# Work woven between attention steps: after every step, or after every other step twice as much at a time

## The chip, the core and the metric

The kernel runs on one core of a Trainium2 chip. A core has five engines that each follow their own list of instructions in order: TensorE (PE in the profile) multiplies matrices, VectorE (DVE) and ScalarE (ACT) work element by element and along rows, GpSimd (POOL) does elementwise work as well, and SyncE (SP) issues the transfers between the main memory and the on-chip memory. TensorE writes its results into PSUM, a small memory that VectorE and ScalarE read from. An instruction waits for the results of other engines through semaphores. The metric is the device time of one execution in microseconds, less is better; the time before is the median of three runs, 1912.97 us (1905.94 to 1915.4).

## What is computed

A two-layer network over 512 latent tokens and 256 context tokens, 1024 channels each. Layer 0 mixes the tokens by attention, layer 1 by a state-space scan in both directions; each is followed by a gated feed-forward part with a short convolution. The change touches the attention of layer 0 alone:

```python
q_l, k_l, v_l = jnp.split(h_lat @ w_qkv, [Q_DIM, Q_DIM + KV_DIM], axis=-1)
q_l = rms_norm(q_l.reshape(bsz, seq, N_HEADS, HEAD_DIM), q_norm)
...
q_l = apply_rope(q_l, cos, sin)
...
s = jnp.einsum('bqhgd,bkhd->bhgqk', q, k).astype(jnp.float32) * (HEAD_DIM ** -0.5)
p = jax.nn.softmax(s, axis=-1).astype(v.dtype)
return jnp.einsum('bhgqk,bkhd->bqhgd', p, v)
...
x = x + mod_l[2] * o_l
```

There are 16 query heads of width 64 and 4 key heads, each shared by four query heads. Latent queries look at all 768 keys, context queries at the 256 context keys. The output goes through a square projection w_o, and before it every sub-layer is normalised and modulated (shift, scale and gate) by a linear map of the conditioning vector.

## The kernel before

Channels lie on the 128 partitions and tokens along the rows. Numbers are f32; a product that needs the precision is made from three products of a high and a low half (`mm3`: high by high, high by low, low by high), so weights are loaded and split into halves first (`load_w`: a transfer, a copy on ScalarE, a difference on VectorE or GpSimd).

Attention (`attention`, from line 379) begins with a stretch whose order is written by hand. It makes the keys and the first four pairs of queries as raw products. The remaining order comes from a scheduler that places instructions engine by engine in keeping with their dependencies; the order in which the program states them is its guide.

Then the heads run in eight pairs (`Pair`), two heads side by side on the two halves of the partitions. A pair has seven steps (`steps`, lines 628 to 690): steps 0 to 5 take the 512 latent queries against one block of 128 keys, step 6 takes the 256 context queries against the two context blocks. Each step has the following parts.

- Scores `ps_s` (lines 673 and 675): three products of halves, and a fourth that subtracts each query's maximum by way of a diagonal matrix `diag`.
- The exponential `pr` on ScalarE (676), which reads the scores out of PSUM, and the running sum `acc` on VectorE (681, 683, 687).
- The values `ps_o` (637), a product of the exponentials with the values. It is stated one step late (`later_lat`, `later_ctx`), so that the next step's scores go ahead of it on TensorE. At the pair's end the sums `ps_sum` or `ps_oc` (643) follow, and three operations on VectorE that divide (648 to 650).

Between these, each step takes one piece of the next pair's `maxima` (lines 591 to 626): a first product `ps_m` (601) whose row maxima VectorE takes (603), to build the next pair's `diag` (619, 624). `ps_s` and `ps_m` take turns in two PSUM buffers of the tag S; each is freed when the exponential or the maximum has read it. All other PSUM results use four buffers of the tag B.

After each step, `fill.run(us)` (line 761) weaves in other work. `Fill` holds a queue of generators; each advances by a small piece when asked and says how many microseconds of TensorE the piece holds, or returns BREAK when its next piece needs something that is still under way. `run` adds its budget to what is left of an overdraft (a surplus is dropped), goes through the queue in order and advances the generators until the budget is used. A generator that returned BREAK cools: it is left out until its count, which goes down by one with each call of `run`, is used up.

The queue holds, in an order written out by hand, the preparation of the queries of pairs 1 to 7 (`queries`), the second half of the keys (`keys`), and six pieces of the modulation (`ada`). A preparation is a product `ps_q` (pairs 4 to 7 only, 105 to 108), then `normed`: squares on ScalarE (528), an exchange of halves by four transfers `qsw` (532), three operations on GpSimd (533 to 535), sums of squares by a matmul with two output columns `ssq` (236), their inverse root on VectorE and ScalarE (239 to 247), transposes `rsTq` (253) and multiplications on VectorE (539), and last the split into halves (85, 87). A BREAK stands between these groups. A modulation piece is a transfer `wada` of four tiles, a product `ps_ada` (128), a copy, and small products with two output columns `ps_adt` (134). At the start of pair p, `fill.require` states whatever is left of the preparation of pair p + 1. At the start of pair 6 the pieces of the output projection (`project`: transfers of w_o, products `ps_d`, sums into X on line 784) are added. The last pair's values go through the projection after the loop.

Of the kernel before, what the change touches and what calls it, by code (L numbers as in the profile page):

```python
# [175 lines left out]
class Fill:  # L176
# [1 line left out]


    def __init__(self):  # L180
        self.q, self.cool, self.left = [], {}, 0.0

    def add(self, gen):
        self.q.append(gen)
# [1 line left out]
    def run(self, us):  # L186

        self.left = min(self.left, 0.0) + us
        self.cool = {g: n - 1 for g, n in self.cool.items() if n > 1}
        for g in list(self.q):  # L190
            while self.left > 0 and g not in self.cool:
                r = next(g, None)
                if r is None:
                    self.q.remove(g)
                    break
                if r is BREAK:
                    self.cool[g] = 3
                    self.left -= 1.0
                else:
                    self.left -= r  # L200
# [178 lines left out]
def attention(g, fill, X, late):  # L379
# [336 lines left out]
    def osplit(p):  # L716
        hl_, hc_ = htiles(g, L, f"ol{p}"), htiles(g, C, f"oc{p}")
        o = g.o[p]
        if p < 6:
            o = t3(g, f"od{p}")  # L720
            nc.sync.dma_start(o, odram[p])
        split(g, o[:, :L], *hl_)
        split(g, o[:, L:T], *hc_)
        g.oT.append((hl_, hc_))
# [15 lines left out]
    for p in range(NH // 2):  # L740
        m = iter(())
        if p < 7:
            fill.require(qgen[p + 1])
            if p == 3:
                fill.require(kgen)
            m = pairs[p + 1].maxima()
        us = 1.75 if p < 6 else 2.9
        for t, todo in enumerate(pairs[p].steps()):
            next(m, None)
            if late_step:  # L750
                late_step()
            late_step = todo
            if t == 0:
                if p == 6:
                    for i in range(5):
                        osplit(i)
                    late()
            if p == 7 and t == 3:
                osplit(5)
                osplit(6)  # L760
            fill.run(us)
    late_step()
    osplit(7)

# [490 lines left out]
def body(nc, tc, I, out, dbg=None):  # L1255
# [47 lines left out]
    def late():  # L1303
        for fs in ((0, 1, 2), (3, 4), (5, 6, 7))[:-1]:
            fill.add(project(fs))

    attention(g, fill, X, late)
    fill.drain()
    g.tables = True
# [136 lines left out]
```

## Time and profile before

| | before |
|---|---|
| time of three runs, median | 1912.97 us |
| time of three runs, lowest and highest | 1905.94 and 1915.4 us |
| time of the profiled execution | 1914.7 us |
| span of the profiled execution, first to last instruction | 1912.9 us |
| mean clock granted to TensorE | 0.994 |
| the heads' loop in the span | 118.4 to 392.5 us |
| executions of the exponential of line 676 (eight pairs, seven steps) | 56 |

The profile is one execution, recorded by the hardware. In a timeline a row gives the start in microseconds, the length, the engine, the line of the kernel, the operation, the result and its sources by the program's names (buffer numbers left out), shapes and how many instructions the row merges; square brackets hold the idle time ahead of the row and what ended it. A row of the table of windows gives the bounds, the width, then the busy time of TensorE's matmuls, of its weight loads, of VectorE, ScalarE and GpSimd, each with its number of instructions, then the granted clock as a share of full speed, the share of the transfer engines and the gigabytes per second. A group of instructions has its count, the busy time in all, the mean length in nanoseconds, and the idle time ahead with what ended it. A matmul of two f32 operands stands in the trace as two. Matmuls are pipelined: a row's length holds its way through the array as well, so the distance from one start to the next is the better measure of what one costs.

### The profile page before, as it was taken

The page shows a single profiled execution, that of the slowest core. Times are in us where ns is not written, and L with a number is a line of the kernel's source. Part 1 is how long each engine was busy: PE and PEld are TensorE (multiplying, and loading weights), DVE is VectorE, ACT ScalarE, POOL GpSimd, SP SyncE. Part 2 cuts the span into 40 slices and gives each one's busy share as a digit, 9 for nine tenths or more (in the row PEclk, how much of TensorE's full clock was granted, in tenths as well). Part 3 has the DMA queues.
Part 4 walks back from the last instruction along what each step waited for, and adds up shares of the span by engine and source line. Part 5 has one row for each costly group of instructions (what it writes and reads, how often), then busy time and mean ns, then how long its engine had stood idle before and what let it go on. Part 6 is the DMA issues. An engine that isn't in the chain of part 4 may idle for free.

```text
span 1912.9 us, 27512 instructions
## 1 busy us (share of the span) xinstructions
PE 1876.5 (98%) x10834; PEld 1547.6 (81%) x10834; DVE 1311.2 (69%) x1943; ACT 823.0 (43%) x1426; POOL 309.8 (16%) x274
## 2 busy tenths in 40 slices
PE   9999999999999999999999999999999999999999
PEld 7866555678888888888888888888888878888887
DVE  5578778678877777444488777777888466565555
ACT  3634444255122222222266777776667352323331
POOL 2241111031000000000040344443434210000000
PEclk9989998999999999999999999999999999999999
DMA  9221332114434555221122443334443322323232
GB/s 337 78 89 45 113 112 95 34 45 166 132 122 132 174 188 166 66 67 60 62 89 87 121 118 115 126 113 133 120 138 115 91 77 86 102 88 110 88 100 88
DMA packets 73425, 210.02 MB, mean 110 GB/s; under 512 B 8912, under 2 KB 14416, under 8 KB 73168
## 3 DMA queue, kind: packets, MB, share of 16 engines
q1 hardware_dynamic: 73296, 208.26, 34.3%
q8 instruction: 85, 1.39, 0.3%
q14 instruction: 44, 0.36, 0.1%
HBM read 198.79 MB, written 6.82 MB: 107 GB/s over the span
## 4 chain that ended last, share of the span: by engine, by line
PE 79%; DVE 9%; issue 3%; ACT 2%; POOL 1%; DMA 1%; DVEq 0%; SPq 0%; POOLq 0%; ACTq 0%
PE ps_up L106 10%; PE ps_up L108 10%; PE ps_up L105 10%; PE ps_d L105 6%; PE ps_d L106 6%; PE ps_d L108 6%; PE ps_in L106 4%; PE ps_in L108 4%; PE ps_in L105 4%; PE ps_o L637 2%; PE ps_s L673 2%; PE ps_st L1033 2%; DVE ht L281 1%; PE ps_wo L108 1%; PE ps_wo L105 1%
## 5 line engine op out<-in xcount | busy, mean ns | idle before, releaser
L87 DVE TENSOR_TENSOR wl<-wst,wh 128x1024 fp32r<-128x1024 f32 x205 | 254.5, 1242 | 244.9 <-PE ps_up L106 137.7
L85 ACT CAST wh<-wst 128x1024 fp32r<-128x1024 f32 x211 | 221.2, 1049 | 423.2 <-DMA wst<-in_wup 333.8
L106 PE MATMUL ps_up<-hlf,wh 128*128 128x512 f32 x1008 | 357.0, 354 | 0.0
L105 PE MATMUL ps_up<-hhf,wh 128*128 128x512 f32 x1008 | 356.9, 354 | 0.0
L108 PE MATMUL ps_up<-hhf,wl 128*128 128x512 f32 x1008 | 356.8, 354 | 0.0
L105 PEld LDWEIGHTS ps_up<-hhf,wh 128*128 128x128 f32 x1008 | 190.5, 189 | 26.5
L106 PEld LDWEIGHTS ps_up<-hlf,wh 128*128 128x128 f32 x1008 | 190.6, 189 | 26.4
L108 PEld LDWEIGHTS ps_up<-hhf,wl 128*128 128x128 f32 x1008 | 190.5, 189 | 26.4
L105 PE MATMUL ps_in<-hhs,wh 128*128 128x512 f32 (+1 forms) x560 | 204.4, 365 | 0.0
L106 PE MATMUL ps_in<-hls,wh 128*128 128x512 f32 (+1 forms) x560 | 199.4, 356 | 0.0
L108 PE MATMUL ps_in<-hhs,wl 128*128 128x512 f32 (+1 forms) x560 | 198.7, 355 | 0.0
L105 PE MATMUL ps_d<-hdh,wh 128*128 128x512 f32 (+1 forms) x568 | 193.6, 343 | 1.4 <-DVE X L784 1.2
L108 PE MATMUL ps_d<-hdh,wl 128*128 128x512 f32 (+1 forms) x568 | 193.5, 341 | 0.0
L106 PE MATMUL ps_d<-hdl,wh 128*128 128x512 f32 (+1 forms) x568 | 193.0, 340 | 0.3 <-DVE hdl L87 0.3
L784 DVE SCALAR_TENSOR_TENSOR X<-ps_d,mod,X 128x512 f32<-128x512 f32 (+1 forms) x224 | 124.6, 583 | 36.9 <-PE ps_d L108 36.6
L106 PEld LDWEIGHTS ps_d<-hdl,wh 128*128 128x128 f32 x568 | 106.6, 188 | 14.8 <-DVE hdl L87 0.7
L105 PEld LDWEIGHTS ps_d<-hdh,wh 128*128 128x128 f32 x568 | 106.3, 188 | 14.8 <-DVE X L784 1.4
L105 PEld LDWEIGHTS ps_in<-hhs,wh 128*128 128x128 f32 x560 | 105.9, 189 | 15.1 <-issue 1.2
L108 PEld LDWEIGHTS ps_in<-hhs,wl 128*128 128x128 f32 x560 | 105.8, 189 | 14.8
L108 PEld LDWEIGHTS ps_d<-hdh,wl 128*128 128x128 f32 x568 | 106.7, 188 | 13.1
L106 PEld LDWEIGHTS ps_in<-hls,wh 128*128 128x128 f32 x560 | 106.0, 189 | 13.2
L676 ACT ACTIVATE pr<-ps_s 128x1024 f32<-128x1024 f32 x56 | 57.2, 1021 | 110.6 <-PE ps_s L675 109.6
(340 smaller groups left out, 3547.3 us busy)
## 6 DMA issues: line engine op xcount, KB each, us to landing
wst<-in_wup SPq DMA_DIRECT2D x88, 512.0 KB, 3.6
wada<-in_adaT SPq DMA_DIRECT2D x56, 512.0 KB, 3.9
wst<-in_win SPq DMA_DIRECT2D x48, 512.0 KB, 3.7
wst<-in_wdown SPq DMA_DIRECT2D x44, 512.0 KB, 3.6
E<-ad SPq DMA_DIRECT2D x64, 256.0 KB, 6.8
wada<-in_adaB SPq DMA_DIRECT2D x24, 512.0 KB, 4.6
ec<-ead SPq DMA_DIRECT2D x64, 128.0 KB, 5.0
wst<-in_wout SPq DMA_DIRECT2D x16, 512.0 KB, 3.6
```

What stands on the lines that cost most here:

```text
L85: keep(nc.scalar.copy(hi, src))
L87: keep(eng.tensor_tensor(lo, src, _r(hi), ALU.subtract))
L105: mm(out, wh, ah, start=first, stop=False)
L106: mm(out, wh, al, start=False, stop=False)
L108: mm(out, wl, ah, start=False, stop=last)
L281: nc.vector.scalar_tensor_tensor(t[:, c0:c1], ap, g.moda[layer][ca][:, m, v : v + 1], rs[:, c0:c1], ALU.mult, ALU.mult)
L637: nc.tensor.matmul(po[S64[e], :n], v, pr[:, 512 * e + off : 512 * e + off + n], start=first, stop=last)
L673: nc.tensor.matmul(outs[e], a[S64[e], k], b[S64[e], q], start=i == 0, stop=False)
L676: nc.scalar.activation(pr, ps, AF.Exp)
L784: nc.vector.scalar_tensor_tensor(ap, o[:, c0:c1], gate[:, m, v : v + 1], ap, ALU.mult, ALU.add)
L1033: nc.tensor.matmul(ps[:, d * 256 : (d + 1) * 256], Bt[:, t * P : (t + 1) * P], xw[d][t], start=t == ts[0], stop=t == ts[-1])
```

## The change

The cooling count becomes a field of the object, 2 in place of 3. In the loop, work is woven in after the steps 1, 3 and 5 of a pair with twice the budget, and after step 6 with the single one; after the steps 0, 2 and 4 none is. The budgets per pair are 7 x 1.75 = 12.25 us in pairs 0 to 5 (3 x 3.5 + 1.75 in the changed kernel) and 7 x 2.9 = 20.3 us in pairs 6 and 7 (3 x 5.8 + 2.9), the same sum both ways. The count goes down with each call of `run`, of which a pair now has four.

```diff
--- before.py
+++ after.py
@@ -178,7 +178,7 @@
     def __init__(self):
-        self.q, self.cool, self.left = [], {}, 0.0
+        self.q, self.cool, self.left, self.pause = [], {}, 0.0, 2
 
@@ -194,7 +194,7 @@
                 if r is BREAK:
-                    self.cool[g] = 3
+                    self.cool[g] = self.pause
                     self.left -= 1.0
@@ -758,7 +758,8 @@
             if p == 7 and t == 3:
                 osplit(5)
                 osplit(6)
-            fill.run(us)
+            if t % 2 or t == 6:
+                fill.run(us if t == 6 else 2 * us)
     late_step()
     osplit(7)
```

## The prediction

> **What bounds the kernel now.** I read the page first, then the busy times of the heads' stretch, then that stretch instruction by instruction on TensorE, ScalarE and VectorE, and last the granted clock in short windows.
>
> ```profile
> span 1912.9 us, 27512 instructions
> PE 1876.5 (98%) x10834; PEld 1547.6 (81%) x10834; DVE 1311.2 (69%) x1943; ACT 823.0 (43%) x1426; POOL 309.8 (16%) x274
> 118.40:392.50 274.10, 270.41 (x1662) 161.08 (x1662) 211.70 (x305) 114.01 (x157) 39.74 (x23) 0.97 0.25 83
> ```
>
> The profiled execution took 1914.7 us, 1.8 us more than its span of 1912.9 us; the median of the three runs is 1912.97 us, 1.7 us below it. I make the sum against this execution and carry the difference to the median. TensorE is busy for 98% of the span. The change acts only between 118.4 and 392.5 us (the last row: eight pairs of heads, seven steps each), where TensorE is busy for 270.4 of 274.1 us. So the woven work fills no large hole; it is itself work of the bounding engine, and its total does not change. What can change is the small change around it: switches between kinds of matmul, waits of a fraction of a microsecond, and the clock, which stands at 0.97 here.
>
> One ordinary step, on TensorE, then the other two engines:
>
> ```profile
> 159.42 0.50 PE L673 MATMUL ps_s<-qh,kh 64*128 64x512 f32 x2
> 160.45 0.40 PE L601 MATMUL ps_m<-kh,qh 64*128 64x512 f32 x2
> 160.77 1.08 PE L637 MATMUL ps_o<-pr,v 128*64 128x512 f32 x4
> 161.78 0.50 PE L105 MATMUL ps_q<-hha,wh 128*128 128x512 f32 x1
> 162.12 0.39 PE L106 MATMUL ps_q<-hla,wh 128*128 128x512 f32 x1
> ...
> 163.73 0.39 PE L108 MATMUL ps_q<-hha,wl 128*128 128x512 f32 x1
> 164.05 0.50 PE L673 MATMUL ps_s<-qh,kh 64*128 64x512 f32 x2
> 160.65 1.02 ACT L676 ACTIVATE pr<-ps_s 128x1024 f32<-128x1024 f32 x1 [3.18 <-PE ps_s L675]
> 160.88 1.23 DVE L603 TENSOR_REDUCE ma<-ps_m 128x2 f32<-128x1024 f32 x1 [0.75 <-PE ps_m L601]
> 162.03 1.21 DVE L683 TENSOR_TENSOR acc<-acc,pr 128x1024 f32<-128x1024 f32 x1
> ```
>
> Scores (ps_s) run from 159.42 to 160.45, the maxima of the next pair (ps_m) to 160.77, the values of the step before (ps_o) to 161.78: 2.36 us. Then come nine woven matmuls (ps_q), and the next scores begin at 164.05. ScalarE's exponential ends at 161.67, VectorE's maximum and sum (1.23 + 1.21) at 163.24.
>
> The clock (third number from the end) in windows cut at its changes, and at one place that has none:
>
> ```profile
> 92.80:96.20 3.40, 2.39 (x19) 1.84 (x18) 2.50 (x4) 2.52 (x3) 0.00 (x0) 1.00 0.00 0
> 96.20:99.70 3.50, 3.50 (x18) 3.50 (x19) 0.99 (x3) 1.29 (x3) 0.00 (x0) 0.51 0.32 77
> 120.10:123.50 3.40, 3.06 (x26) 2.49 (x25) 2.96 (x4) 3.27 (x6) 3.40 (x3) 1.00 0.50 155
> 123.50:130.40 6.90, 6.90 (x29) 2.54 (x29) 5.50 (x9) 3.26 (x6) 0.80 (x1) 0.51 0.44 125
> 178.10:181.50 3.40, 3.40 (x22) 2.32 (x19) 3.28 (x8) 1.04 (x3) 2.08 (x2) 1.00 0.00 0
> 287.40:290.80 3.40, 2.98 (x22) 2.09 (x20) 3.23 (x2) 1.06 (x2) 3.35 (x2) 1.00 1.02 399
> 291.00:301.30 10.30, 10.30 (x39) 6.09 (x39) 6.88 (x12) 3.29 (x5) 2.17 (x1) 0.51 0.27 105
> 294.20:297.60 3.40, 3.40 (x17) 3.38 (x18) 2.60 (x5) 0.28 (x1) 0.00 (x0) 0.50 0.00 0
> 96.00:97.00 1.00, 1.00 (x7) 1.00 (x7) 1.00 (x2) 0.00 (x0) 0.00 (x0) 0.62 0.26 61
> 123.00:124.00 1.00, 1.00 (x7) 1.00 (x8) 1.00 (x1) 1.00 (x2) 1.00 (x1) 0.77 0.00 0
> 290.00:291.00 1.00, 0.38 (x6) 0.01 (x2) 1.00 (x2) 0.00 (x0) 0.94 (x1) 0.90 1.02 399
> ```
>
> It is full or half. The mean of 0.62 from 96 to 97 puts the first drop at 97 − 0.38/0.5 = 96.24; in the same way the others begin at 123.54 and 290.80. The 27.30 and 167.26 us between them are 8 and 49 times 3.41 us; they last about 3.4, 6.9 and 10.2 us, that is 1, 2 and 3 such periods. So in this trace the clock is set anew every 3.41 us. What went ahead of each drop:
>
> ```profile
> 93.84 0.50 PE L601 MATMUL ps_m<-kh,qh 64*128 64x256 f32 x4 [1.01 <-ACT qh L85]
> 95.14 1.75 PE L236 MATMUL ssq<-cst,qsq 128*128 128x2 f32 x12
> 119.80 1.50 PE L236 MATMUL ssq<-cst,qsq 128*128 128x2 f32 x12
> 122.99 2.24 PE L236 MATMUL ssq<-cst,qsq 128*128 128x2 f32 x12 [0.34 <-ACT qsq L528]
> 178.75 1.50 PE L236 MATMUL ssq<-cst,qsq 128*128 128x2 f32 x12
> 287.74 1.50 PE L236 MATMUL ssq<-cst,qsq 128*128 128x2 f32 x12
> 290.99 0.80 PE L601 MATMUL ps_m<-kh,qh 64*128 64x256 f32 x4 [0.62 <-DVE ma L603]
> 293.62 3.58 PE L134 MATMUL ps_adt<-cst,ada_sb 128*128 128x2 f32 x16
> ```
>
> Matmuls with two output columns (ssq, the sums of squares; ps_adt, the turned modulation rows) stream almost nothing. Counted with the idle time, the periods before the drops hold 1.01 + 1.10 = 2.1, 1.1 + 0.34 + 0.55 = 2.0 and 1.43 + 0.43 = 1.86 us of near-idleness (a group of twelve ssq takes 1.43, from 119.80 to the next matmul at 121.23). The period from 178.15 holds one such group and is followed by no drop. The threshold lies between 1.43 and 1.86 us of 3.41.
>
> **The change part by part.** The built order of the changed kernel holds the same work in the stretch; it stands elsewhere. I count 18 steps with nothing woven in (the first, third and fifth of a pair mostly) against 2 before, so 16 new light steps, and as much more work in the heavy ones.
>
> *The switch.* A change of the kind of matmul costs the first one extra: the first ps_q takes 162.12 − 161.78 = 0.34 where a following one takes 0.23 (+0.11); the last ps_q holds until 164.05, 0.32 for 0.23 (+0.09). A light step saves both and pays one switch from values to scores (estimated +0.10, the mean of the two). 16 x −0.10 = −1.6 us; between 0 and −3.2.
>
> *A light step by itself.* Without the nine matmuls the next scores begin at 2.36 + 0.09 = 2.45 us after the last. Their bank was freed by the exponential, 161.67 − 159.42 = 2.25 us after: covered by 0.2. The next maxima need the bank that VectorE's maximum freed at 162.11, 2.69 us after, and come at 2.45 + 1.03 = 3.48: covered by 0.79. VectorE needs 2.3 us (start to start) of 2.45. So a light step runs without a wait as long as no more than about 0.8 us of woven work stands on VectorE ahead of its maximum. One step has no values to cover it: the first of all.
>
> ```profile
> 119.68 1.02 ACT L676 ACTIVATE pr<-ps_s 128x1024 f32<-128x1024 f32 x1 [0.75 <-PE ps_s L675]
> ```
>
> There the sums of squares stood behind the maxima (119.80, above); in the changed order the second scores follow at once and wait for the exponential to 120.70: +0.9 us.
>
> *VectorE's backlog.* Present waits of the maxima for VectorE:
>
> ```profile
> 138.95 0.50 PE L601 MATMUL ps_m<-kh,qh 64*128 64x512 f32 x2 [0.48 <-DVE mb L603]
> 306.97 0.50 PE L601 MATMUL ps_m<-kh,qh 64*128 64x256 f32 x4 [0.55 <-DVE ma L603]
> L601 PE MATMUL ps_m<-kh,qh 64*128 64x256 f32 (+1 forms) x140 | 21.3, 342 | 2.5 <-DVE ma L603 2.1 <-DVE mb L603 0.5
> ```
>
> Each is about 0.5 us, 2.5 us in all. Twice as much woven work at a time can put its normalisation in front of the light step's maximum, and no woven matmul covers TensorE then. Bounds: none of the 16 waits (0) and all wait 0.5 us (8.0). I take a third, +2.6 us, nearer the low end: in most steps the scheduler has put the normalisation behind the maximum.
>
> *The clock.* Before, the two drops cost 6.9 x 0.49 = 3.4 and 10.2 x 0.5 = 5.1, together 8.5 us. The first goes: the two ssq groups that shared a period now have a light step, or scores, between them (2.9 us of work from end to start), so with the 1.43 us of one group no period reaches 1.86. The second goes as it was, but all twelve ps_adt matmuls of the sixth pair (24 in the trace, two for each) now stand in one row: at 0.12 us each (the ssq group, 12 in 1.43) 2.9 us without streaming. Wherever the period's edge falls, it holds at least 1.65 us of them in about 9 of 10 cases. That drop lasts one or two periods: 1.7 or 3.4 us, I take 2.6. For ssq groups that meet a new wait I add 0.4 of a two-period drop, 1.4 us. Sum after 4.0, so −4.5 us; bounds −8.5 (no drop) and +8.5 (two-period drops at five places, 17.0).
>
> The Trainium skill, "TensorE: Matmul & The Clock Gate", section "HAM oscillation — how this bites in real kernels", has the abstract rule that only idle gaps over about 3.4 us bring the half clock; here the longest gap before a drop was 1.01 us, so the trace does not follow it. Its section "A second HAM failure mode: psum-queue depth-cycling" says that frequent micro-idling between groups of matmuls is enough, which speaks against this change; the trace agrees as far as 1.86 us in 3.41 goes.
>
> *Later preparation.* The cool time is now 2 runs of every second step, so 3 to 4 steps instead of 3, and the last pair's sums of squares move from the sixth pair's third step to its sixth, all its transposes to the seventh. Behind them stand VectorE's multiplications, ScalarE's high half of the queries, and the maxima of the last pair; behind these the scores that need the same banks.
>
> ```profile
> 306.83 0.68 DVE L539 TENSOR_TENSOR qs<-qs,rsTq 128x512 f32<-128x512 f32 x1
> 309.98 0.42 DVE L539 TENSOR_TENSOR qs<-qs,rsTq 128x256 f32<-128x256 f32 x1
> 310.61 0.81 ACT L85 CAST qh<-qs 128x768 fp32r<-128x768 f32 x1
> wst<-in_w_o SPq DMA_DIRECT2D x8, 512.0 KB, 4.5
> ```
>
> The chain is 0.68 + 0.42 + 0.81 = 1.9 us if nothing stands between, against scores and values of one step as cover, 1.03 + 1.01; but the pair's own closing work on VectorE stands between. Bounds 0 and 2.4 (one maximum and one sum ahead of the chain, 1.2 us each); I take +1.0. On SP's queue five of the last projection's loads now stand ahead of that pair's exchange of halves, which the multiplications need. One behind another they would take 5 x 4.5 = 22 us; the steps three to six that lie between are about 14 (2.9 of ps_adt and 1.43 of ssq on four steps of 2.45). They overlap, so I take nothing, and 8 us in the range.
>
> From the last step of the last pair on the order is the same on every engine, so no later stage should change in length.
>
> Sum: −1.6 + 0.9 + 2.6 − 4.5 + 1.0 = −1.6 us. 1914.7 − 1.6 = 1913.1 for a profiled execution, 1911 us for the median.
>
> **The rivals.**
> 1. *VectorE's backlog decides (slower).* Place: the maxima of the 16 light steps. Each waits 0.5 to 1 us and the waits join with ssq into more slow periods. Price: 8.0 (all wait 0.5) in place of 2.6, and three more two-period drops, 10.2: 1911 + 5.4 + 10.2 = 1927. It passes 0.5% (1922.5) from a mean wait of 0.88 us without more drops (16 x 0.88 = 14.1, 11.5 more than my 2.6), or 0.5 us with two more. For it: VectorE has 2.3 us of work in a step of 2.45, and is busy 211.7 of 274.1 us already. Against it: the 0.79 us of cover, and present steps that are uneven already, with 2.5 us of such waits in all.
> 2. *No drop at all (faster).* The rows of ps_adt count as activity, or are broken up by the edge. −1.6 + 0.9 − 8.5 = −9.2 with no backlog, and −11.7 if the present 2.5 us go as well: 1901 to 1904. For it: 178.1 shows that 1.43 us are borne. Against it: 294.20, a period full of ps_adt and scores, stayed at half. By the rule of the Trainium skill quoted above (no gap near 3.4 us) it would come out this way.
> 3. *Late preparation shows at every pair's end.* 7 x 1.0 us in place of 1.0: 1917. Against it: in the first, fifth and sixth pair the last transposes stand in the last step before as after.
> 4. *The change does little of what it says,* because the scheduler pulls woven matmuls back between the scores (it does so in the first and third pair): near 1913, inside the forecast.
>
> **How the numbers follow.** 0.5% of 1912.97 is 9.6 us, about what a measurement of this kernel can tell from no change; the three runs differ by as much. The forecast with rival 4 has 0.45, rival 3 0.12 (both within), rival 1 0.26 (all slower), rival 2 0.17 (counted as faster). The likeliest's own range is 1904 to 1919. The range of eighty in a hundred reaches to most of both outer cases: 1901 to 1926.
>
> **What would show it.** Right: in the heads' stretch light steps of 2.4 to 2.7 us and heavy ones of 5 to 8; no half clock around 123 us, and one of 3.4 or 6.8 us behind the row of ps_adt; waits of the maxima for VectorE of about 5 us in all; the stretch within 3 us of 274. Wrong: waits of the maxima over 10 us, more than two half-clock stays, scores that wait for the exponential in many steps (the cover of 0.2 us is thin), or a stage after 392 us that changes length.

## The result and the profile after

The changed kernel takes 1916.34 us (median of 20 runs, 1912.01 to 1921.7), the kernel before 1909.21 us (median of the 20 runs beside them). One of those 20 took 3066.82 us; the ratio compares fast runs alone. It is 1.0038, 95% interval [1.0028, 1.0048]: slower by 0.38%, about 7 us. That lies inside the predicted range and inside the 0.5% called no change, but the forecast of a small gain has the wrong sign.

The page of the profile after (its time is 1918.66 us, 1.8 us more than its span):

```profile
span 1916.9 us, 27524 instructions
PE 1875.7 (98%) x10834; PEld 1550.7 (81%) x10834; DVE 1314.3 (69%) x1943; ACT 823.7 (43%) x1426; POOL 309.6 (16%) x274
```

TensorE still bounds the kernel, with as much work as before. The window of the heads' stretch, after the change (columns as in the prediction):

```profile
118.50:395.40 276.90, 268.00 (x1662) 161.93 (x1661) 213.68 (x305) 114.38 (x157) 39.31 (x24) 0.98 0.25 82
```

The stretch is longer by 2.8 us (276.9 for 274.1) though its clock is better (0.98 for 0.97): it loses 5.1 us to half clock where the one before lost 8.5. Without these it is 6.2 us longer. Behind the stretch TensorE runs the same list in both kernels. One row of it, before and after:

```profile
1538.99 0.51 PE L105 MATMUL ps_first<-hhf,wh 128*128 128x256 f32 x2 [0.64 <-ACT hhf L290]
```

```profile
1541.85 0.50 PE L105 MATMUL ps_first<-hhf,wh 128*128 128x256 f32 x2 [0.64 <-ACT hhf L290]
```

The kernel after is 2.86 us late here and 4.00 us late at the last matmul (1913.33 for 1909.33). So the later stages take the same time but for 1.14 us, and these come from a drop of the clock close behind this row, which the profile before does not have. Two periods of 3.41 us before, then two after:

```profile
103.07:106.48 3.41, 1.62 (x16) 1.56 (x15) 3.41 (x3) 0.00 (x0) 0.97 (x1) 1.00 0.00 0
1540.07:1543.48 3.41, 2.12 (x16) 1.71 (x15) 3.41 (x5) 1.78 (x6) 2.34 (x2) 1.00 0.31 123
```

```profile
1540.93:1544.34 3.41, 2.02 (x11) 1.20 (x9) 3.41 (x8) 3.05 (x7) 0.82 (x1) 1.00 0.52 160
1544.34:1547.75 3.41, 2.72 (x12) 2.73 (x13) 3.41 (x8) 1.79 (x5) 1.51 (x2) 0.50 0.00 0
```

The same three waits (0.64, 0.26 and 1.03 us) stand here in both kernels, but the periods cut them at other places: the period from 1540.07 before holds 1.29 us without a matmul and full clock follows; that from 1540.93 after holds 1.39 us, and two periods at half clock follow. The period from 103.07, to which the text comes back, holds 1.79 us, and full clock follows it. The mean granted clock of the whole execution is 0.994 in both profiles, 11.5 us lost in each.

In TensorE's timeline the light steps look as forecast:

```profile
262.54 0.51 PE L673 MATMUL ps_s<-qh,kh 64*128 64x512 f32 x2
264.92 0.49 PE L673 MATMUL ps_s<-qh,kh 64*128 64x512 f32 x2
266.87 0.51 PE L601 MATMUL ps_m<-kh,qh 64*128 64x256 f32 x4 [0.76 <-DVE ma L603]
270.17 0.50 PE L673 MATMUL ps_s<-qh,kh 64*128 64x512 f32 x2
```

The scores of one light step begin at 262.54, the next at 264.92, 2.38 us later. The next step has work woven in and takes 5.25 us, with a wait for VectorE's maximum (0.76 us) in it. The idle times in such brackets, summed over TensorE's rows from the first exponential to 3 us after the last, come to 8.85 us in 12 waits after, and to 3.36 us in 8 waits before. The largest of them have these causes.

ScalarE, ahead of its exponential (timeline of TensorE and ScalarE):

```profile
120.88 0.50 PE L673 MATMUL ps_s<-qh,kh 64*128 64x512 f32 x2 [0.88 <-ACT pr L676]
...
173.30 0.94 ACT L529 ACTIVATE qs<-qs,qn 128x768 f32<-128x768 f32 x1
175.19 0.50 PE L673 MATMUL ps_s<-qh,kh 64*128 64x512 f32 x2 [0.70 <-ACT pr L676]
...
194.51 0.83 ACT L550 CAST kh<-raw 64x768 fp32r<-64x768 f32 x1 [2.58 <-DVE raw L539]
195.37 0.83 ACT L551 CAST kh<-raw 64x768 fp32r<-64x768 f32 x1
196.21 0.83 ACT L550 CAST kh<-raw 64x768 fp32r<-64x768 f32 x1
197.06 0.83 ACT L553 CAST kl<-kl 64x768 fp32r<-64x768 f32 x1
197.92 1.02 ACT L676 ACTIVATE pr<-ps_s 128x1024 f32<-128x1024 f32 x1
198.99 0.50 PE L673 MATMUL ps_s<-qh,kh 64*128 64x512 f32 x2 [1.40 <-ACT pr L676]
```

The first row is the stretch's second scores (0.88 us). The next two are a step of the second pair with almost nothing woven in: ScalarE worked on the preparation of queries (line 529) and began the exponential only at 174.14, and the scores waited 0.70 us. The third wait can be followed: the scores ended about 196.3 and were ready for the exponential, but ScalarE had four casts and copies of the second key half in its queue (0.83 us each, without a gap), began the exponential at 197.92, and the next scores, which need that buffer, started 1.40 us late.

VectorE, ahead of its maximum, and the change from the sixth pair to the seventh:

```profile
222.95 2.04 DVE L87 TENSOR_TENSOR ql<-qs,qh 128x768 fp32r<-128x768 f32 x1
224.91 1.21 DVE L603 TENSOR_REDUCE ma<-ps_m 128x4 f32<-128x1024 f32 x1
226.17 0.51 PE L601 MATMUL ps_m<-kh,qh 64*128 64x512 f32 x2 [1.73 <-DVE ma L603]
...
316.12 0.51 PE L675 MATMUL ps_s<-diag,onesr 64*128 64x512 f32 x2 [0.62 <-DVE diag L624]
317.75 1.07 PE L637 MATMUL ps_o<-pr,v 128*64 128x512 f32 x2 [1.12 <-ACT pr L676]
```

A split of 2.04 us stands ahead of the maximum of 224.91, and the next maxima wait 1.73 us. At the pair's end the scores wait 0.62 us for the diagonal, and the values behind them another 1.12 us for the exponential.

The second loss is no wait at all. It is seen where the two column halves of a value product are torn apart:

```profile
136.69 1.07 PE L637 MATMUL ps_o<-pr,v 128*64 128x512 f32 x2
137.69 1.05 PE L128 MATMUL ps_ada<-wada,sc 128*32 128x512 f32 x4
138.67 1.07 PE L637 MATMUL ps_o<-pr,v 128*64 128x512 f32 x2
139.67 0.50 PE L673 MATMUL ps_s<-qh,kh 64*128 64x512 f32 x2
```

In the step that the prediction quotes, both halves (x4: two heads, two passes each) ran from 160.77 to 161.78, 1.01 us. Here the scheduler has put half a modulation product between them: one half takes 1.00 us from start to start, the other 1.00 as well. Side by side the two take as long as one alone; torn apart each takes the whole time. The modulation product has the same trouble: its x8 ran from 134.34 to 135.34, half of it (x4, 137.69) takes 0.98. The built order of the stretch holds 4 torn value pairs and 2 torn modulation groups after the change, 2 and 1 before.

The clock, in windows of one period of 3.41 us:

```profile
144.87:148.28 3.41, 2.80 (x28) 2.46 (x28) 3.41 (x3) 0.98 (x1) 1.26 (x1) 1.00 0.77 191
148.28:151.69 3.41, 3.41 (x15) 1.73 (x16) 2.48 (x7) 0.05 (x1) 0.00 (x0) 0.50 0.33 121
196.07:199.48 3.41, 2.01 (x14) 0.72 (x12) 2.60 (x4) 3.32 (x5) 0.00 (x0) 1.00 0.00 0
223.38:226.79 3.41, 1.68 (x15) 0.91 (x12) 3.41 (x4) 1.02 (x1) 3.33 (x3) 1.00 0.00 0
226.79:230.20 3.41, 3.41 (x16) 3.31 (x17) 3.29 (x4) 0.34 (x1) 0.67 (x1) 0.50 0.29 115
298.47:301.88 3.41, 3.41 (x30) 2.94 (x32) 1.97 (x7) 1.53 (x3) 0.00 (x0) 1.00 0.35 81
315.54:318.95 3.41, 1.71 (x6) 0.58 (x8) 3.23 (x8) 2.54 (x4) 0.00 (x0) 1.00 0.01 2
318.95:322.36 3.41, 3.41 (x15) 1.82 (x14) 2.89 (x5) 1.22 (x2) 0.00 (x0) 0.50 0.18 67
```

```profile
145.19 1.05 PE L134 MATMUL ps_adt<-cst,ada_sb 128*128 128x2 f32 x8
297.41 2.84 PE L134 MATMUL ps_adt<-cst,ada_sb 128*128 128x2 f32 x24
```

The second fence has two rows of TensorE's timeline. There are three stays at half clock in the stretch, one period each, 5.1 us lost against 8.5 before; more than two was one of the prediction's signs of being wrong. The period behind that from 196.07 is at full clock. The drop at 123 us is gone; the row of 24 ps_adt from 297.41, which was to bring one, did not (298.47 to 305 stays at full).

### The profile page after: what moved, and what is told of

It is laid out like the page before. It is cut to its first block, busy times and chain, and to the rows that moved or that the text cites. A ratio compares the mean times of both kernels' runs of the same rounds, so it can differ in the third digit from the quotient of the medians.

```text
span 1916.9 us, 27524 instructions
## 1 busy us (share of the span) xinstructions
PE 1875.7 (98%) x10834; PEld 1550.7 (81%) x10834; DVE 1314.3 (69%) x1943; ACT 823.7 (43%) x1426; POOL 309.6 (16%) x274
## 3 DMA queue, kind: packets, MB, share of 16 engines
q8 instruction: 85, 1.39, 0.3%
## 4 chain that ended last, share of the span: by engine, by line
PE 78%; DVE 10%; issue 3%; ACT 2%; POOL 1%; DMA 1%; DVEq 0%; POOLq 0%; ACTq 0%
PE ps_up L106 10%; PE ps_up L108 10%; PE ps_up L105 10%; PE ps_d L105 6%; PE ps_d L106 6%; PE ps_d L108 6%; PE ps_in L108 4%; PE ps_in L106 4%; PE ps_in L105 4%; PE ps_o L637 2%; PE ps_s L673 2%; PE ps_st L1034 2%; DVE ht L281 1%; PE ps_wo L108 1%; DVE xf L964 1%
## 5 line engine op out<-in xcount | busy, mean ns | idle before, releaser
L106 PEld LDWEIGHTS ps_in<-hls,wh 128*128 128x128 f32 x560 | 106.0, 189 | 13.2
L167 DVE SCALAR_TENSOR_TENSOR junk<-wada,cb 128x1024 f32<-128x1024 f32 x80 | 97.6, 1220 | 1.2 <-ACT cb L159 0.9
```

The source lines that it names most:

```text
L106: mm(out, wh, al, start=False, stop=False)
L167: g.tc.keep_in_program_order(nc.vector.scalar_tensor_tensor(junk, w, 1.0, cb[:, v * D : (v + 1) * D], ALU.mult, ALU.mult, accum_out=md[:, ...
```

## The experiments

Where a run has its clock drops depends on how the program meets the 3.41 us periods, as the drop behind 1540.93 shows, and a period at half clock counts as 1.7 us lost, so single executions of one kernel differ by several microseconds. For every run I therefore take the *drop-free span* as well, the span times the granted clock, and average it over all runs of a kernel; the mean scatters by about half a microsecond (± is one standard error of the kernel's own runs). It also has an error that no averaging takes out: it counts every half-clock stay at half its length, but the 6.8 us behind 1544.34 delayed the later stages by 1.14 us and not by 3.4; 0.69 us of its first period (3.41 less 2.72) are idle anyway. "Lost" is the rest. "Idle" is the sum of TensorE's waits in the stretch of the profiled execution, "torn" the torn value pairs plus torn modulation groups in the built order. The "sum" is worked out: idle less 3.4, plus 1.0 for each torn one over 3, less 1.6 where the weaving alternates (16 light steps of 0.10 us).

| kernel | median us | ratio to before | lost | drop-free, against before | idle | torn | sum |
|---|---|---|---|---|---|---|---|
| before, again | 1910.77 | 1.0008 [0.9997, 1.002] | 9.2 | 0.0 ± 0.5 | 3.4 | 3 | 0 |
| after | 1916.34 | 1.0038 [1.0028, 1.0048] | 8.4 | +6.5 ± 0.4 | 8.85 | 6 | +6.9 |
| pause_only | 1909.89 | 1.0 [0.9991, 1.001] | 10.2 | -1.9 ± 0.4 | 3.6 | 1 | -1.8 |
| weave_only | 1933.18 | 1.013 [1.0115, 1.0145] | 14.3 | +18.2 ± 0.9 | 20.4 | 7 | +19.4 |
| third | 1941.52 | 1.0169 [1.0152, 1.0187] | 20.9 | +19.7 ± 0.3 | 21.6 | 10 | +23.6 |
| after_keys | 1917.89 | 1.0028 [1.0017, 1.0038] | 9.3 | +6.1 ± 0.3 | 8.8 | 6 | +6.8 |
| even | 1917.09 | 1.0024 [1.0013, 1.0034] | 11.3 | +3.4 ± 0.5 | 8.8 | 3 | +3.8 |
| before_swap | 1934.15 | 1.0107 [1.009, 1.0124] | 17.4 | +13.0 ± 0.6 | 8.3 | 3 | +4.9 |
| after_swap | 1946.16 | 1.0175 [1.0162, 1.0188] | 21.4 | +22.0 ± 0.3 | 17.2 | 4 | +13.2 |
| alt_whole | 1913.68 | 1.0012 [1.0, 1.0024] | 12.7 | -1.8 ± 0.4 | 7.6 | 0 | -0.4 |
| alt_torn | 1931.16 | 1.0108 [1.0091, 1.0125] | 12.3 | +16.5 ± 0.7 | 9.1 | 13 | +14.1 |
| each_whole | 1911.45 | 1.0002 [0.9991, 1.0013] | 10.7 | -2.0 ± 0.3 | 5.5 | 0 | -0.9 |
| weave_later | 1924.23 | 1.0066 [1.0043, 1.0089] | 12.5 | +8.7 ± 0.5 | 10.9 | 6 | +8.9 |

The kernels before beside them had a mean drop-free span of 1899.8 us in the first batch (before_again, weave_only, pause_only, third; after, run ahead of it, is set against this too) and 1900.7 in the two later ones; they lost 7.9, 10.1 and 8.7 us. Against 1900.7, after would stand at +5.6. In the two profiles alone the stretch is 6.2 us longer without its half-clock time, as said above.

**The kernel before, once more** (before_again; no edit).

> The kernel before once more, to have the granted clock beside every run's span. With a mean clock c, span x (1 - c) is the time that half-clock periods cost; the span less that is the span without drops. The changed kernel's 20 runs give 1905 to 1908 us for it (1910.8 at clock 0.998, 1917.5 at 0.995). Theory A (the changed kernel loses by waits in its light steps, behind ScalarE and VectorE): here the span without drops is about 1901 to 1903, 5 us less, and the mean clock about 0.996 to 0.997, like the changed kernel's 0.996. Theory B (the loss is the clock): the span without drops is 1905 to 1908 here too, and the mean clock is 0.998 or higher. A second profile should show fewer or shorter half-clock stays than the first one's 17 us in the heads' stretch, since the median run is 5.5 us faster than the profiled one.

Its drop-free span is that of the other runs, 1899.8 us. Its twelve runs lost between 3.8 and 15.3 us, the mean is 9.2 ± 0.9; the twenty runs of the changed kernel lost 3.8 to 13.4, mean 8.4 ± 0.7. So the clock is no measurable part of the difference, and theory B falls. And the 1914.7 us from which the prediction was made (11.5 us lost, at 0.994) was a draw from the upper half. One expectation failed: the second profile has as much half clock in the stretch as the first (17.1 us), again with 6.8 us from 123 us on, but the rest at other places (3.4 us from 181 us, 6.8 us from 297 us, where the first had 10.2 us from 291 us).

**Half of the change each** (weave_only: the new weaving, cooling still 3; pause_only: every step, cooling 2).

```diff
-        self.q, self.cool, self.left, self.pause = [], {}, 0.0, 2
+        self.q, self.cool, self.left, self.pause = [], {}, 0.0, 3
```

> The weaving after every other step as in the changed kernel, the cooling count 3 as before. Theory A (waits of the light steps): as slow as the changed kernel, +0.25 to +0.55% of before (1914 to 1920 us), with 7 us or more of TensorE idle in the heads' stretch (3.4 before, 8.8 changed). Theory C (the later preparation, that is the pair of cooling and fewer runs, does it): 3 counts at four runs a pair cool longer than 2, so worse than the changed kernel, +0.6% or more. Theory B: no fixed order, the clock decides.

```diff
-                    self.cool[g] = 3
+                    self.cool[g] = 2
```

> Weaving after every step as before, the cooling count 2 in place of 3. Theory A: no light steps (3 in the built order), so within 0.2% of before (1906 to 1913 us), TensorE idle 3 to 5 us. Theory C (the cooling count matters by itself): away from before by more than 0.25%.

The shorter cooling by itself costs nothing (ratio 1.0); drop-free it is 1.9 us shorter, with 1 torn in place of 3. The weave_only run took 1933 us where theory A had at most 1920: theory C had the direction (over 0.6%). The weaving without the shorter cooling costs much more than the change as a whole, and TensorE's timeline shows the chief reason, 8.25 of its 20.4 us of idle time:

```profile
157.07 1.92 PE L128 MATMUL ps_ada<-wada,sc 128*32 128x512 f32 x4 [4.72 <-DMA wada<-in_adaB]
162.52 1.92 PE L128 MATMUL ps_ada<-wada,sc 128*32 128x512 f32 x4 [3.53 <-DMA wada<-in_adaB]
```

SyncE's, for the transfers of that product:

```profile
152.44 12.37 SPq L122 DMA_DIRECT2D wada<-in_adaB  x4
```

The four transfers are issued from 152.44 on, and the product that needs them is next on TensorE's list from 152.35 (157.07 less 4.72) on. It waits 4.72 and 3.53 us for them. By the program's text it comes about like this: with a cooling of 3 all preparations cool at once, the double budget goes down the queue to a modulation piece, and states its product in the very run that stated its transfers. The run weave_later below tests this.

**Three steps at a time** (third).

```diff
-            if t % 2 or t == 6:
-                fill.run(us if t == 6 else 2 * us)
+            if t in (2, 5, 6):
+                fill.run(us if t == 6 else 3 * us)
```

> The dose: woven work after steps 2 and 5 with three budgets and after step 6 with one, cooling count 2; 24 light steps in the built order in place of 18. Theory A: more waits than in the changed kernel, 10 to 16 us of TensorE idle in the heads' stretch, +0.5 to +1.0% of before (1919 to 1928 us). Theory B: time follows the clock alone, so near the changed kernel's 1916 with no more idle than its 8.8 us.

The waits grow with it, as theory A has it, but beyond its range (21.6 us for 10 to 16, and 1941.5 us for 1919 to 1928); 7.1 of them are again for the modulation's transfers. With three steps at a time a cooling of 2 doesn't avoid them.

**The modulation's product later** (weave_later: weave_only, and a piece that has stated its transfers cools too).

```diff
+LATER = object()
...
-                if r is BREAK:
+                if r is BREAK or r is LATER:
                     self.cool[g] = self.pause
-                    self.left -= 1.0
+                    self.left -= 1.0 if r is BREAK else 0.0
...
-    yield 0
+    yield LATER
```

> The alternate weaving with the cooling count left at 3 (it took 18 us more than before, 8.25 us of its idle time in the modulation product that waited for its transfers), with one thing added: a modulation piece that has just stated its transfers cools as well, without a charge to the budget, so that its product comes at least three runs later. Theory A (the product was stated too soon behind its own transfers): the waits of ps_ada for transfers fall from 8.25 us to below 1, and the drop-free span from before + 18 to before + 10 or less. Rival (the wait is one for a queue that is full, or goes to whatever stands next): the idle time stays within 3 us of 20.4 and the span with it.

No wait for those transfers is left, the idle time falls from 20.4 to 10.9 us and the drop-free span from +18.2 to +8.7. This is the chief part that the shorter cooling plays in the change: it avoids this wait.

**ScalarE relieved** (after_keys: the key copies of the lines 551 and 553 become transfers; the casts of line 550 stay).

```diff
-            nc.scalar.copy(h[o], qs[s])
+            nc.sync.dma_start(_r(h)[o], _r(h)[s])
...
-            nc.scalar.copy(l[o], _r(l)[s])
+            nc.sync.dma_start(_r(l)[o], _r(l)[s])
```

> The changed kernel, with the four copies of the keys to the other half of the partitions (lines 551 and 553, 0.83 us each) made by transfers instead of ScalarE; TensorE's order is the changed kernel's. Theory A (waits of the light steps, ScalarE's part): the 1.40 us wait of the scores for the exponential at 199 us, behind four such casts, goes; span without drops 1904.5 to 1905.5 us where the changed kernel has 1906.3. If ScalarE's queue had nothing to do with it, the span without drops stays at 1906.3 and a wait stays at that place.

The wait of 1.40 us is gone, but the total is 8.8 us as before. A new one stands at another place (timeline of ScalarE and TensorE):

```profile
126.76 0.21 ACT L241 ACTIVATE rsy<-rsa 128x12 f32<-128x12 f32 x1 [3.84 <-DVE rsa L239]
127.00 0.21 ACT L241 ACTIVATE rsy<-rsy 128x12 f32<-128x12 f32 x1
127.12 1.01 ACT L676 ACTIVATE pr<-ps_s 128x1024 f32<-128x1024 f32 x1
128.18 0.50 PE L673 MATMUL ps_s<-qh,kh 64*128 64x512 f32 x2 [1.31 <-ACT pr L676]
```

So the wait at 199 us was ScalarE's, but the expected gain (1904.5 to 1905.5 us) did not come: 1906.8. Now two small operations of an inverse root stand ahead of the exponential. ScalarE sat idle for 3.84 us before the first of them, waiting for VectorE's sums (rsa), with the exponential queued behind it. In both places TensorE paid for what stood ahead of the exponential on ScalarE, work in the one and a wait in the other; taking one such piece away brought no measurable gain (drop-free +6.1 ± 0.3 for +5.6 to +6.5).

**The other steps light** (even: work after the steps 0, 2, 4 and 6).

```diff
-            if t % 2 or t == 6:
+            if t % 2 == 0:
```

> Woven after the steps 0, 2 and 4 with twice the budget and after 6 with one, so that the light steps are 1, 3 and 5; cooling count 2. In the built order 20 light steps and none of the two heads' value matmuls torn apart (4 in the changed kernel, 2 before). Theory A2 (light steps as such cost by their waits): span without drops 1904 to 1908, near the changed kernel's 1906.3. Theory D (not the light steps, but where the scheduler tore value matmuls apart, 1.0 us each, and the uncovered first step): 1900 to 1902, near before's 1899.8.

The order has no torn value pair and 3 torn modulation groups. It idles as long as the changed kernel, yet its drop-free span is 2 to 3 us shorter, 1904.0 us. That is the lower edge of theory A2 and outside theory D's 1900 to 1902, so it decides for neither alone. With 3 torn fewer it is a first sign that torn pairs count.

**The values stated ahead of the maxima** (before_swap, after_swap).

```diff
-            next(m, None)
             if late_step:
                 late_step()
+            next(m, None)
             late_step = todo
```

> The same exchange in the kernel before. It has 3.4 us of TensorE idle, 2.6 of it at the maxima behind VectorE: at most 2.6 us less than its 1899.8 us without drops (1897 to 1900); a larger gain would say that the exchange helps by something else than VectorE's waits.

> The changed kernel, with the values of the step before stated ahead of the next pair's maxima, so that VectorE has 1.0 us longer to free the maxima's bank. 2 torn pairs of value matmuls in the built order in place of 4. Theory A (VectorE's part: 0.41, 1.73, 0.76 and 0.15 us of waits of the maxima in the changed kernel): these go, 3 us, and up to 2 us of torn matmuls: span without drops 1901.5 to 1903.5 in place of 1906.3. If VectorE's backlog is not what they wait for: 1906 or more.

Both failed by far (1913.7 and 1922.7 us drop-free). In after_swap the maxima's waits for VectorE did fall, from 3.05 to 1.78 us, but others came in their place: 17.2 us in all, 4.4 of them at the scores for the diagonal and 3.4 at a modulation product. Beside the waits and the torn ones, 8.1 and 8.8 us stay open. A step of before_swap on TensorE:

```profile
168.94 0.39 PE L675 MATMUL ps_s<-diag,onesr 64*128 64x512 f32 x2
169.26 1.08 PE L637 MATMUL ps_o<-pr,v 128*64 128x512 f32 x4
170.27 0.50 PE L601 MATMUL ps_m<-kh,qh 64*128 64x512 f32 x2
170.70 0.65 PE L253 MATMUL rsTq<-cst,rbq 128*128 128x128 f32 x4
```

and one of the kernel before:

```profile
168.12 0.39 PE L675 MATMUL ps_s<-diag,onesr 64*128 64x512 f32 x2
168.35 0.40 PE L601 MATMUL ps_m<-kh,qh 64*128 64x512 f32 x2
168.68 1.08 PE L637 MATMUL ps_o<-pr,v 128*64 128x512 f32 x4
169.69 0.66 PE L253 MATMUL rsTq<-cst,rbq 128*128 128x128 f32 x4
```

Scores and maxima have the same shape, values another. From the last scores' start to the woven work it takes 1.57 us before (168.12 to 169.69) and 1.76 in the swapped order (168.94 to 170.70), 0.19 more; of 27 such steps of before_swap at full clock, 25 lie between 1.75 and 1.79. The order "scores, values, maxima, woven work" has one change of shape more than "scores, maxima, values, woven work". It shows at both of its sides: the last scores hold 0.32 us in place of 0.23, and the maxima 0.43 (170.27 to 170.70) in place of 0.33. So a change costs about 0.1 us on the product ahead of it and 0.1 on the one behind. In after_swap a light step has no more changes than in after, as the next scores follow the maxima at once.

Added up from start to start over the stretch, without waits and with half-clock time at half its length, scores and maxima take 6.1 us more in before_swap than in before, and 5.9 us more in after_swap than in after. That is the larger part of the 8.1 and 8.8 us; the rest is spread over other products. It measures the switch of the prediction (estimated 0.10) in another place.

**Whole and torn, at the same weaving** (alt_whole, alt_torn: only the cooling and the budget move, and the scheduler's order with them).

```diff
-        self.q, self.cool, self.left, self.pause = [], {}, 0.0, 2
+        self.q, self.cool, self.left, self.pause = [], {}, 0.0, 1
...
-        us = 1.75 if p < 6 else 2.9
+        us = 1.7 if p < 6 else 2.9
```

> Weaving after the steps 1, 3, 5 and 6 as in the changed kernel, but a cooling count of 1 and a budget of 1.7 us in place of 1.75: in the built order no pair of value matmuls and no group of four modulation matmuls is torn apart (changed kernel: 4 and 2; before: 2 and 1). The drop-free span is the span times its granted clock. Theory A (three terms make up the difference to the kernel before: idle time of TensorE in the heads' stretch, 1.0 us for each torn pair or group, -1.6 us for the light steps): drop-free span = before - 3 - 1.6 + (its idle time - 3.4), so +1.6 us against before if it idles 9.6 us as the changed kernel does. Theory B (torn pairs cost nothing, idle time is all): +4.6 us at the same idle time. Theory C (weaving after every other step costs by itself): +6.5 us as the changed kernel. Median time by A about 1912, by B 1915, by C 1917, where before is about 1910.

```diff
-        us = 1.75 if p < 6 else 2.9
+        us = 1.9 if p < 6 else 2.9
```

> The same places of weaving, cooling count 2 and a budget of 1.9 us in place of 1.75: the built order has 10 torn pairs of values and 3 torn groups of modulation matmuls. Theory A: drop-free span = before + 10 - 1.6 + (its idle time - 3.4), that is +14.6 us at 9.6 us of idle time. Theory B: +4.6 us at the same idle time. Theory C: +6.5 us. Read against alt_whole, A has 13 us between the two besides their idle time, B none.

(The 9.6 us of idle time in these texts counts one wait of the changed kernel twice; it is 8.85.) One row of the groups of instructions, that of the value products, in alt_whole and alt_torn; the columns are the busy time and the mean of one:

```profile
L637 PE MATMUL ps_o<-pr,v 128*64 128x512 f32 x192 | 51.8, 618 | 0.0
```

```profile
L637 PE MATMUL ps_o<-pr,v 128*64 128x512 f32 x192 | 64.5, 640 | 0.0
```

The same 192 instructions keep TensorE busy 51.8 us with no pair torn and 64.5 us with ten torn, 1.3 us each with the half-clock stays in it. With their idle time at 7.6 and 9.1 us the two differ by 18.4 us drop-free; theory A's sum gives 14.5, B's 1.5, and C's none. B and C fall. A is right in kind; some 4 us of the difference it does not hold. The two traces, added up from start to start as above, show where they stand: the values take 8.8 us more in alt_torn, the modulation's products 3.3, the sums `ps_sum` 1.0 (one of their pairs is torn too, which the count leaves out), scores, maxima and transposes 4.9, the waits 1.5. A matmul put between two halves also adds changes of shape; whether these are the 4.9 us, no run tells.

The same sum for before and after, 6.2 us in the profiled stretch: waits +5.5, values +2.4 and modulation +1.1 (torn apart), the woven products `ps_q` and `ps_d` -3.9, scores, context values and transposes +1.1, all others +0.1. In before and after the values row itself says less (56.4 and 57.5 us busy), because it holds the half-clock time, of which before has more in the stretch.

**Whole, after every step** (each_whole: cooling 2, budget 1.8).

```diff
-                    self.cool[g] = 3
+                    self.cool[g] = 2
...
-        us = 1.75 if p < 6 else 2.9
+        us = 1.8 if p < 6 else 2.9
```

> Weaving after every step as before, cooling count 2, budget 1.8 us: no torn pair and no torn group. Theory A: 3 us less than before at the same idle time (3.4 us), a drop-free span of about 1897 where before has 1900, a ratio of 0.998. Theory B: as before, ratio 1.0 within 0.001. If it idles more than 3.4 us, the surplus comes on top in both.

It idles 2.1 us more than before and is still 2.0 us shorter drop-free, which is A's side (its sum is -0.9) and not B's. But its runs lost 10.7 us to the clock, those of before 8.7, and the ratio is 1.0002 [0.9991, 1.0013]. alt_whole is the plainer case: 7.5 to 8.3 us better than the changed kernel drop-free, 4 us of it given back to the clock (12.7 lost for 8.4 to 8.7). None of these versions beats the kernel before by what can be measured.

## Why the prediction was wrong

The range held, and the sum without its clock term, +2.9 us, had the right sign. Step by step:

- *The clock, -4.5 us: the step that failed.* "Before, the two drops cost 6.9 x 0.49 = 3.4 and 10.2 x 0.5 = 5.1, together 8.5 us. The first goes." The first did go: both profiles of the kernel before have a drop at 123 us, those of after and after_keys have none. In the profiled stretch the loss fell by 3.4 us (8.5 to 5.1). But the whole execution lost as much as before (11.5 us at 0.994 in both), since a drop came behind 1540.93 in a stage that the change does not touch; and averaged over runs there is no gain (8.4 ± 0.7 lost after; 7.9 ± 0.5, 9.2 ± 0.9, 10.1 ± 0.5 and 8.7 ± 0.6 before). Taking the drops of one trace in one stretch for a cost of that order was the mistake: it turned a small loss into a small gain.
- *The rule for a drop.* "The threshold lies between 1.43 and 1.86 us of 3.41." The traces follow no such threshold. Of idle time alone, the periods from 223.38 and 315.54 hold 3.41 - 1.68 = 1.73 and 1.70 us and are followed by half clock, and that from 196.07 with 1.40 is not; but that from 1540.93 with 1.39 is, and in the kernel before that from 103.07 with 1.79 is not. With matmuls of two columns it is no clearer: the period from 298.47 holds 1.71 us of the row of ps_adt (to 300.18) and is not followed by a drop, while 0.61 us of idle time with 0.98 of ps_adt (from 144.87) is. What the clock counts stays open. The Trainium skill, "TensorE: Matmul & The Clock Gate", section "HAM oscillation — how this bites in real kernels", allows gaps up to about 3.4 us; again the trace does not agree, with 1.73 us as the longest gap in the stretch.
- *Torn pairs, not in the sum: +3.0 us.* The prediction counted the woven matmuls as work that merely stands elsewhere ("its total does not change"). Three more torn pairs and groups at 1.0 us each are three microseconds of additional time on the engine that bounds; from start to start the values and the modulation's products take 3.5 us more. It is the second step that failed, a term put at nothing. The same page of the Trainium skill, section "Part 3: Packing small matmuls — row/col tiling", says that matmuls on different tiles of the array overlap and that matmuls never overtake one another; the rows agree with the overlap (1.01 us for both halves side by side, 1.00 for one alone). With a matmul of another kind between them, the rows show no overlap of the halves.
- *A light step by itself.* Right in length (2.38 us for 2.45) and for the first one (0.88 us for +0.9). Wrong in what was behind "covered by 0.2": the text asked only what stands ahead of VectorE's maximum and put ScalarE's other work at nothing. That work stood ahead of the exponential in two such steps, +2.1 us (0.70 and 1.40).
- *VectorE's backlog, +2.6 us.* Mis-sized: the maxima wait 3.05 us in all for VectorE (0.41, 1.73, 0.76 and 0.15), 2.55 before; +0.5. Rival 1 is refuted.
- *Later preparation, +1.0 us.* The change to the seventh pair costs 0.62 + 1.12 us, and small waits of the preparation elsewhere 1.08; before, such waits came to 0.81. So +2.0. Rival 3 foresaw the time (1917), but not by its mechanism: one pair's end shows, not seven.
- *The switch, -1.6 us.* Right in sign, too small in size. From start to start the woven products take 3.9 us less, and scores, context values and transposes 1.1 more, so -2.8 us, near the bound of -3.2. The prediction let a light step pay one switch from values to scores (+0.10). But the first scores take 0.34 us behind values (264.92 to 265.26) as behind woven work (262.54 to 262.88): a light step saves both switches, 0.20 us, and pays none.
- *Later stages.* The same order and the same length, as forecast, but for the 1.14 us of the drop behind 1540.93.

Together, with the prediction's -1.6 and the estimate of 3.0, -1.6 + 5.5 (0.9 + 2.1 + 0.5 + 2.0) + 3.0 = +6.9 us; with the terms as the traces show them, -2.8 + 5.5 + 3.5 = +6.2. Measured are +5.6 to +6.5. The forecast for the waits as a whole was +4.5. So from -1.6 to +6.9 the missing gain of the clock makes 4.5 us, the torn pairs 3.0 and the waits 1.0; that 4.5 came near 5.5 is partly luck, as VectorE's share was far too large and ScalarE's missing. What remains open: why the clock loss of some orders is larger (alt_whole 12.7, third 20.9, after_swap 21.4 us); more waits go with more loss, but alt_whole idles less than after and loses more. No run tells this apart. Nor is it shown why scores, maxima and transposes take longer in alt_torn than in alt_whole.

## What to carry to other kernels

Where an engine is busy for 98%, moving its work about still changes its time: products that share the array should stay side by side (1.0 us for each pair torn here), a change of shape has its price (about 0.2 us here), and a step without filler must be covered on each of the engines it hands work to, not on one. Clock drops of one trace are no fixed cost of the order; average them over runs, or take them out of span and time, before they enter a sum. A weaving budget and a cooling count belong together: the shorter cooling alone gained nothing in the measured time, but with work after every other step it kept a product from being stated right behind its own transfers.

## What the hardware showed that was not expected

- Half a value product (64 of 128 columns of the array) alone takes 1.00 us, both halves side by side 1.01. The difference over a kernel is plain in one row: 51.8 against 64.5 us for the same 192 instructions.
- A change of shape between scores and values costs TensorE about 0.1 us on each of its sides. One change more in a step is 0.19 us, and scores and maxima take 6.1 us more over the stretch of before_swap.
- Idle time alone does not tell when TensorE falls to half clock: periods of 3.41 us with 1.39, 1.70 and 1.73 us of it were followed by half clock, others with 1.29, 1.40 and 1.79 were not. The same waits, 2.86 us later, brought a drop in one kernel and none in the other. The same kernel loses 3.8 us in one run and 15.3 us in another.
